# Weight splits written five half units ahead, expert output written in its own expert, and a pinned end

## The chip, the cores and the metric

The kernel runs on one core of one Trainium2 chip. The metric is the time of one execution on the device, in microseconds (us); three executions were timed, and their median counts. Engines are named as in the profile: PE is TensorE (PEld its weight loads), DVE is VectorE, ACT is ScalarE, POOL is GpSimd, SP is SyncE, which issues DMAs.

## The reference

One encoder block on x of 1024 positions by 1024 channels, in float32. A mixer (Fourier groups beside a gated short convolution) comes first; the change does not touch it. Then 16 experts follow, each of which takes the 128 positions with its highest router probability:

```python
probs = softmax(h @ w_router + b_router)
vals, idx = top_k(swapaxes(probs, 1, 2), 128)      # per expert: 128 positions
xe = h[idx]                                        # 128 x 1024
a = xe @ w_gate_e ; u = xe @ w_up_e                # 1024 x 2048 each
y = (silu(a) * u) @ w_down_e                       # 2048 x 1024
x[idx] += gate_f * (y * vals)
return rms_norm(x, g_final)
```

Weights are 25 MB an expert, and each is used once.

## The kernel before, in words

The kernel is written in a framework that plans the order of each engine when the kernel is built: a list scheduler walks through planned time, and among the instructions whose inputs and buffers are ready in the plan the one that was written first goes first. On the chip each engine then runs its own list in that order, and semaphores make it wait for others. `issue_after(i)` tells the planner that what is written inside comes after i in its engine's order.

Experts run one after the other (`expert`, L1176). An expert has 24 weight units of 1 MB: `raw` tiles of 128 x 2048, fetched by SP (`fetch`, L1107, issue at L1120) in a fixed list (`ulist`) into a ring of 7 + 4 + 1 = 12 buffers; the next unit is fetched when one has been split. A unit has two halves of 128 x 1024. Each half is split for precision (`split`, both lines recorded as L92 and L93): ACT copies it rounded into `whi` (L92), DVE subtracts for the rest, `wlo` (L93). Both have six buffers (`NWB`). A half is then used by 6 or more matmuls on TensorE of 512 columns: hi x hi, hi x lo, lo x hi (L1300 to L1302 for a and u, L106 to L112 for y).

The order in which an expert is written: for each of four column blocks fc, `up` (L1185) makes a of 512 columns from four halves, `put` (L1200) transposes the former block's product (L1205) and splits it into hth and htl, `up` makes u, then Silu of a (L1243, ACT) and the product h (L1244, DVE); in block 1 the next expert is chosen (`pick`: one-hot oh on DVE L1068, eight small matmuls L1075, the gather on POOL L1087); `down` (L1218) adds the former block's part to y. `unit` (L1147) writes the two instructions of a half's split right in front of that half's matmuls. At the end `turn` transposes the next expert's gathered rows (L1104). The weighed output ys (L1269, DVE) and its scatter with add to x2 in memory (L1270, POOL) are kept in a list, `self.left`, and written inside the next expert's first `up`, after its first unit.

The last expert has three units that are used unsplit in float32 (`plain`, matmuls L1222), with the transposed product copied into `htf` (L1209). Instead of scattering, it reads its rows of x2 early, and other rows of x2 are fetched as four more units at the places of `FIN` in the list; each is normed and written out (`final`: squares on ACT L1313, fms on DVE L664, frs on POOL L666, scaling on DVE L1318). The end group (L1282 to L1295) makes the last y in three column groups: h0 to h2 (L1286), add0 to add2 into xg (L1287), squares on ACT (L1288), gl0 to gl2 with g_final (L1289), the sum (L1291), ems and ers (L664, L666), the scaling and the output.

Of the kernel before, what the change touches and what calls it, by code (L numbers as in the profile page):

```python
# [6 lines left out]
F32 = mybir.dt.float32  # L7
# [4 lines left out]
OP = mybir.AluOpType  # L12
# [15 lines left out]
NWS, NWB = 3, 6  # L28
NSH = 0
NCMP = 2  # L30
FIN = ((10, 0), (8, 2), (6, 4), (4, 6))


def host_tables():
# [46 lines left out]
class Block:  # L81
# [575 lines left out]
            for _ in range(n):  # L657
                self.nc.tensor.matmul(t[:, 0:P], lhsT=self.ident, rhs=self.ident, start=True, stop=True)

    def rstd(self, pool, ss, name):  # L660
        nc = self.nc
        n = ss.shape[1]
        ms = pool.tile([P, n], F32, name=name + "ms")
        nc.vector.tensor_scalar(ms, ss, 1.0 / D, EPS, op0=OP.mult, op1=OP.add)  # L664
        rs = pool.tile([P, n], F32, name=name + "rs", bufs=2)
        nc.gpsimd.tensor_tensor(rs, ms, self.neghalf[:, 0:n], op=OP.pow)  # L666
        return rs

    def posdft(self, pool, v, row, cos, r, m, nm):

# [468 lines left out]
    def plain(self, rows):  # L1139

        raw = self.take().rearrange("p (i k n) -> p i k n", i=2, k=rows // 2)
        for i in range(2):
            yield raw[:, i]
            if i:
                self.fetch()
            self.step()

    def unit(self, rows):

        raw = self.take()  # L1150
        nc = self.nc
        for i in range(2):
            hi = self.wsp.tile([P, 1024], F32R, name="whi")
            lo = self.wsp.tile([P, 1024], F32R, name="wlo")
            src = raw[:, 1024 * i:1024 * i + 1024]
            if self.npop < NWS:
                nc.scalar.activation(hi, src, AF.Copy)
                with self.tc.issue_after(self.after):
                    nc.vector.tensor_tensor(lo, src, hi, op=OP.subtract)
            elif self.npop < NWB:  # L1160
                with self.tc.issue_after(self.hold):
                    self.split(hi, lo, src)
            else:
                self.split(hi, lo, src)
            self.npop += 1
            if i:
                if self.npop <= NWS:
                    with self.tc.issue_after(self.gather):
                        self.fetch(nc.gpsimd)
                else:  # L1170
                    self.fetch()
            self.pin = self.last
            self.step()
            yield hi.rearrange("p (k n) -> p k n", k=rows // 2), lo.rearrange("p (k n) -> p k n", k=rows // 2)

    def expert(self, pool, e, picked, side):  # L1176

# [7 lines left out]
        def up(fc, name):  # L1185
            ps = self.pau.tile([P, 512], F32, name=name)
            k = 0
            for b in range(2):
                for j, (wh, wl) in enumerate(self.unit(4)):
                    if self.npop > NWB and (j == 0 or self.ranked < 2):  # L1190
                        with self.tc.issue_after(self.hold):
                            next(side, None)
                    for i in range(2):
                        self.mm3x(ps, (xh[:, k, :], xl[:, k, :]), (wh[:, i, :], wl[:, i, :]), k == 0, k == KD - 1)
                        k += 1
                if self.left:
                    self.left.pop()()
            return ps

        def put(fc):  # L1200

            pt = self.ptp.tile([P, 4, P], F32, name="tp")
            h = hs.pop(fc)
            for i in range(4):
                nc.tensor.transpose(pt[:, i, :], h[:, i * P:(i + 1) * P], self.ident)  # L1205
            hf = None
            if last and fc in (1, 2):
                hf = pool.tile([P, 4, P], F32, name="htf")
                nc.scalar.activation(hf, pt, AF.Copy)  # L1209
                if fc == 2:  # L1210
                    ht[fc] = (None, None, hf)
                    return
            hh = pool.tile([P, 4, P], F32R, name="hth", bufs=2)
            hl = pool.tile([P, 4, P], F32R, name="htl", bufs=2)
            self.split(hh, hl, pt)
            ht[fc] = (hh, hl, hf)

        def down(fc, b):  # L1218
            if last and (fc, b) in ((1, 1), (2, 0), (2, 1)):
                for i, w in enumerate(self.plain(2)):  # L1220
                    for n in (0, 512):
                        nc.tensor.matmul(y[:, n:n + 512], lhsT=ht[fc][2][:, 2 * b + i, :], rhs=w[:, 0, n:n + 512],  # L1222
                                         start=False, stop=False)
                return
            for i, (wh, wl) in enumerate(self.unit(2)):
                if i == 0:
                    next(side, None)
                f = 4 * fc + 2 * b + i
                self.mm3([y[:, 0:512], y[:, 512:1024]], [t[:, 2 * b + i, :] for t in ht[fc][0:2]],
                         [(wh[:, 0, n:n + 512], wl[:, 0, n:n + 512]) for n in (0, 512)],  # L1230
                         first=(f == 0), last=(f == 15))

        for fc in range(4):
            pa = up(fc, "a")
            if last and fc == 0:
                self.gl = pool.tile([P, D], F32, name="ys")
                nc.gpsimd.dma_start(out=self.gl, in_=self.io["g_final"].rearrange("(o d) -> o d", o=1)
                                    .partition_broadcast(P))
            if fc:
                put(fc - 1)  # L1240
            pu = up(fc, "u")
            h = pool.tile([P, 512], F32, name="h", bufs=2)
            nc.scalar.activation(h, pa, AF.Silu)  # L1243
            nc.vector.tensor_tensor(h, pu, h, op=OP.mult)  # L1244
            hs[fc] = h
            if fc == 1:
                if last:
                    xg = pool.tile([P, D], F32, name="xg")
                    nc.gpsimd.indirect_dma_start(out=xg, out_offset=None, in_=self.x2_d,
                                                 in_offset=bass.IndirectOffsetOnAxis(ap=idx[:, 0:1], axis=0))  # L1250
                else:
                    while self.ranked < e + 2:
                        next(side, None)
                    with self.tc.issue_after(self.after):
                        nxt = self.pick(pool, e + 1)
            if fc:
                down(fc - 1, 0)
                if fc == 3:
                    put(3)
                down(fc - 1, 1)  # L1260
# [3 lines left out]
        if not last:  # L1264
            down(3, 1)

            def add():
                ys = pool.tile([P, D], F32, name="ys")
                nc.vector.scalar_tensor_tensor(ys, in0=y, scalar=val, in1=self.gf, op0=OP.mult, op1=OP.mult)  # L1269
                nc.gpsimd.indirect_dma_start(out=self.x2_d,  # L1270
                                             out_offset=bass.IndirectOffsetOnAxis(ap=idx[:, 0:1], axis=0),
                                             in_=ys, in_offset=None, compute_op=OP.add)
                self.scattered = e == NE - 2

            self.left.append(add)
            return nxt
        w = list(self.unit(2))
        for _ in range(8):
            self.step()
        ss = pool.tile([P, 3], F32, name="sse")  # L1280
        for n, cs in enumerate((slice(0, 512), slice(512, 768), slice(768, 1024))):
            for i, (wh, wl) in enumerate(w):  # L1282
                self.mm3x(y[:, cs], [t[:, 2 + i, :] for t in ht[3][0:2]], (wh[:, 0, cs], wl[:, 0, cs]), False, i == 1,
                          skip_group_check=n == 2)
            h = pool.tile([P, 512], F32, name="h", bufs=2)[:, 0:cs.stop - cs.start]
            nc.vector.scalar_tensor_tensor(h, in0=y[:, cs], scalar=val, in1=self.gf[:, cs], op0=OP.mult, op1=OP.mult)  # L1286
            nc.vector.tensor_tensor(xg[:, cs], xg[:, cs], h, op=OP.add)  # L1287
            nc.scalar.activation(h, xg[:, cs], AF.Square, accum_out=ss[:, n:n + 1])  # L1288
            nc.vector.tensor_tensor(xg[:, cs], xg[:, cs], self.gl[:, cs], op=OP.mult)  # L1289
        st = pool.tile([P, 1], F32, name="sst")  # L1290
        nc.vector.tensor_reduce(st, ss, axis=AX.X, op=OP.add)  # L1291
        rs = self.rstd(pool, st, "e")
# [31 lines left out]
    def run(self):  # L1324
# [92 lines left out]
        for i, t in FIN:  # L1417
            self.ulist.insert(len(self.ulist) - i, (None, NE - 1, P * t, P * t + 256, 0, D))
        self.nfetch, self.npop, self.units, self.rows = 0, 0, [], []
        def last():  # L1420
            return self.merge_out(m, KD - 1, *mg)

# [49 lines left out]
        side = self.route_rest(mp)  # L1472
        picked = self.turn(mp, *picked)
        self.hold = self.turned
        self.left = []
# [25 lines left out]
```

## Time and profile before

| what | value |
|---|---|
| median of 3 runs | 1948.76 us (1948.51 to 1949.74) |
| profiled execution | 1944.46 us, its span 1942.6 us, mean granted clock 0.992 |
| PE / PEld / DVE / ACT / POOL busy, share of the span | 97% / 78% / 82% / 58% / 7% |
| raw weights, issue to landing, median | 7.2 us (gate), 9.1 (up), 8.1 (down), 1 MB each |
| DMA | 549.02 MB, 283 GB/s over the span |

The experts begin at 775.76 us of the span. A matmul's record overlaps the next one's, so the busy share of PE is not its use. PEclk is the granted clock of TensorE as a share of full speed; a wait is shown in brackets behind an instruction, with the one that ended it.

### The profile page before, as it was taken

To read this page: it belongs to the slowest core of one execution; us is meant where nothing else is said; L and a number is where in the kernel's file an instruction comes from. 1 tells how busy PE (TensorE), PEld (TensorE's weight loads), DVE (VectorE), ACT (ScalarE), POOL (GpSimd) and SP (SyncE) were. 2 spreads that over 40 slices of the span, in tenths; PEclk is the share of its full clock that TensorE was granted. 3 is DMA by queue.
4 is the path that set the end of the run, shared out by engine and by line. 5 is a ranking of instruction groups with operands and counts; after the bars stand their busy time and mean duration, and the time that the engine had idled before them with its cause. 6 is when DMAs were issued, how large, how long until landed. Compare 5 with 4: busy or idle time off the path is not lost.

```text
span 1942.6 us, 23945 instructions
## 1 busy us (share of the span) xinstructions
PE 1888.7 (97%) x8777; PEld 1507.7 (78%) x8777; DVE 1583.4 (82%) x2005; ACT 1117.6 (58%) x1403; POOL 136.2 (7%) x124
## 2 busy tenths in 40 slices
PE   6999999999999999999999999999999999999996
PEld 5788888777788877777888777777778778777873
DVE  5976678676853767999999898898998999989886
ACT  5533233433510433776787777777767777677764
POOL 1000000000130111000000000000000000000001
PEclk9999999999999999999999999999999999999998
DMA  8322224465774842999999999999999999999993
GB/s 298 128 67 65 87 76 154 143 228 195 232 250 140 291 180 108 396 367 346 378 372 389 354 359 376 372 364 360 392 364 355 386 366 361 380 373 355 392 367 135
DMA packets 244746, 549.02 MB, mean 283 GB/s; under 512 B 12644, under 2 KB 51652, under 8 KB 244628
## 3 DMA queue, kind: packets, MB, share of 16 engines
q1 hardware_dynamic: 229248, 494.50, 69.8%
q0 software_dynamic: 14528, 52.75, 8.6%
q8 instruction: 69, 1.13, 0.2%
q10 hardware_dynamic: 852, 0.24, 0.1%
q14 instruction: 49, 0.40, 0.1%
HBM read 507.61 MB, written 39.86 MB: 282 GB/s over the span
## 4 chain that ended last, share of the span: by engine, by line
PE 76%; DVE 12%; DMA 5%; issue 4%; ACT 2%; POOL 0%; ACTq 0%; POOLq 0%; DVEq 0%
PE pb L315 9%; DVE wlo L93 7%; PE pa L315 6%; PE pc L315 6%; PE u L1302 5%; PE u L1300 5%; PE u L1301 5%; PE y L106 5%; PE y L109 4%; PE y L112 4%; PE a L1302 4%; PE a L1301 4%; PE a L1300 4%; DMA raw<-in_w_up_e_dram 3%; PE mm L106 3%
## 5 line engine op out<-in xcount | busy, mean ns | idle before, releaser
L93 DVE TENSOR_TENSOR wlo<-raw,whi 128x1024 fp32r<-128x1024 f32 x759 | 889.0, 1218 | 61.1 <-ACT whi L92 52.5
L92 ACT ACTIVATE whi<-raw 128x1024 fp32r<-128x1024 f32 x759 | 751.4, 1052 | 61.2 <-PE y L112 21.6
L1302 PE MATMUL a<-wlo,xh 128*128 128x512 f32 x512 | 206.2, 403 | 7.0 <-DVE wlo L93 5.7
L1302 PE MATMUL u<-wlo,xh 128*128 128x512 f32 x512 | 203.6, 398 | 2.4 <-DVE wlo L93 2.4
L1300 PE MATMUL u<-whi,xh 128*128 128x512 f32 x512 | 202.5, 395 | 1.6 <-ACT whi L92 1.6
L1300 PE MATMUL a<-whi,xh 128*128 128x512 f32 x512 | 201.5, 394 | 1.9 <-ACT whi L92 1.6
L1301 PE MATMUL a<-whi,xl 128*128 128x512 f32 x512 | 201.8, 394 | 0.0
L1301 PE MATMUL u<-whi,xl 128*128 128x512 f32 x512 | 201.8, 394 | 0.0
L109 PE MATMUL y<-wlo,hth 128*128 128x512 f32 x496 | 161.3, 406 | 0.5 <-DVE wlo L93 0.3
L106 PE MATMUL y<-whi,hth 128*128 128x512 f32 x496 | 159.5, 402 | 0.0
L112 PE MATMUL y<-whi,htl 128*128 128x512 f32 x496 | 156.4, 396 | 0.0
L92 ACT ACTIVATE wh<-s 128x512 fp32r<-128x512 f32 x80 | 50.3, 631 | 135.9 <-PE pc L315 76.0
L1302 PEld LDWEIGHTS a<-wlo,xh 128*128 128x128 f32 x512 | 96.4, 188 | 39.3 <-DVE wlo L93 19.8
L1302 PEld LDWEIGHTS u<-wlo,xh 128*128 128x128 f32 x512 | 96.3, 188 | 31.1 <-DVE wlo L93 8.0
L1300 PEld LDWEIGHTS a<-whi,xh 128*128 128x128 f32 x512 | 96.7, 189 | 21.9 <-ACT whi L92 2.5
L1301 PEld LDWEIGHTS a<-whi,xl 128*128 128x128 f32 x512 | 96.5, 188 | 22.0 <-DVE xl L93 0.4
L1300 PEld LDWEIGHTS u<-whi,xh 128*128 128x128 f32 x512 | 96.5, 188 | 21.0 <-ACT whi L92 2.6
L1301 PEld LDWEIGHTS u<-whi,xl 128*128 128x128 f32 x512 | 96.6, 189 | 20.5
L112 PEld LDWEIGHTS y<-whi,htl 128*128 128x128 f32 x496 | 93.4, 189 | 22.5
L106 PEld LDWEIGHTS y<-whi,hth 128*128 128x128 f32 x496 | 91.8, 189 | 20.9 <-issue 0.5
L109 PEld LDWEIGHTS y<-wlo,hth 128*128 128x128 f32 x496 | 89.9, 190 | 20.4 <-DVE wlo L93 2.4
L1243 ACT ACTIVATE h<-a 128x512 f32<-128x512 f32 x64 | 38.2, 596 | 106.6 <-PE a L1302 106.6
(530 smaller groups left out, 3183.1 us busy)
## 6 DMA issues: line engine op xcount, KB each, us to landing
raw<-in_w_gate_e_dram SPq DMA_DIRECT2D x126, 1024.0 KB, 7.2
raw<-in_w_up_e_dram SPq DMA_DIRECT2D x126, 1024.0 KB, 9.1
raw<-in_w_down_e_dram SPq DMA_DIRECT2D x126, 1024.0 KB, 8.1
ld<-in_w_ada_dram SPq DMA_DIRECT2D x48, 512.0 KB, 5.4
ld<-in_w_in_dram SPq DMA_DIRECT2D x44, 512.0 KB, 4.4
sg_d<-q POOLq DMA_DIRECT2D x8, 1024.0 KB, 6.1
ld<-sg_d SPq DMA_DIRECT2D x16, 512.0 KB, 4.9
x<-in_x_dram SPq DMA_DIRECT2D x8, 512.0 KB, 3.3
```

Of the source, the lines that this page charges most:

```text
L92: a = self.nc.scalar.activation(hi, src, AF.Copy).ins
L93: self.last = a, self.nc.vector.tensor_tensor(lo, src, hi, op=OP.subtract).ins
L106: nc.tensor.matmul(o, lhsT=lh, rhs=rh, start=first, stop=False)
L109: nc.tensor.matmul(o, lhsT=lh, rhs=rl, start=False, stop=False)
L112: nc.tensor.matmul(o, lhsT=ll, rhs=rh, start=False, stop=last)
L315: nc.tensor.matmul(o, lhsT=x[:, k, :], rhs=y[:, k, :], start=first and k == 0 and i == 0, stop=last and k == 3 and i == 2, skip_group_chec ...
L1243: nc.scalar.activation(h, pa, AF.Silu)
L1300: nc.tensor.matmul(o, lhsT=lhs[0], rhs=rhs[0], start=first, stop=False, **kw)
L1301: nc.tensor.matmul(o, lhsT=lhs[1], rhs=rhs[0], start=False, stop=False, **kw)
L1302: nc.tensor.matmul(o, lhsT=lhs[0], rhs=rhs[1], start=False, stop=last, **kw)
```

## The change

- `half` and `unit`: splits are written ahead of use. A queue takes halves until six stand in it, so five half units are written in front of the matmuls of a half. Plain halves stand in the queue too; `free` fetches the next unit in the order of the list of units.
- Silu of a is written right after a, in front of `put` and of u.
- ys and the scatter are written at the end of their own expert; `self.left` is gone.
- `htf` has two buffers.
- `FIN`: the first three of the four units of rows come 2, 1 and 1 units later in the list; `PICK` and `PLAIN` name values that are the same as before.
- In the end group the DVE operations are pinned in the order h0, add0, gl0, h1, add1, gl1, h2, add2, sum, ems, gl2.

```diff
-FIN = ((10, 0), (8, 2), (6, 4), (4, 6))
+PICK = 1
+FIN = ((8, 0), (7, 2), (5, 4), (4, 6))
+PLAIN = ((1, 1), (2, 0), (2, 1))
...
+    def half(self):
...
+        rows, plain = self.plan[self.nunit]
+        i = self.nhalf
+        if i == 0:
+            self.raw = self.take()
+        src = self.raw[:, 1024 * i:1024 * i + 1024]
+        if plain:
+            parts = [src]
...
+        self.queue.append([x.rearrange("p (k n) -> p k n", k=rows // 2) for x in parts])
+        if i:
+            if not plain:
+                self.free(self.nunit)
+            self.nunit += 1
+        self.nhalf = 1 - i
+        self.step()
...
+    def free(self, n):
+
+        self.read.add(n)
+        while self.nfree in self.read:
+            self.nfree += 1
+            if self.nfree == 1:
+                with self.tc.issue_after(self.gather):
+                    self.fetch(self.nc.gpsimd)
+            else:
+                self.fetch()
+
+    def unit(self):
+
+        for i in range(2):
+            while len(self.queue) < NWB and self.nunit < len(self.plan):
+                self.half()
+            self.nused += 1
+            yield self.queue.pop(0)
...
-                if self.left:
-                    self.left.pop()()
...
-                hf = pool.tile([P, 4, P], F32, name="htf")
+                hf = pool.tile([P, 4, P], F32, name="htf", bufs=2)
...
             pa = up(fc, "a")
+            h = pool.tile([P, 512], F32, name="h", bufs=2)
+            nc.scalar.activation(h, pa, AF.Silu)
...
             pu = up(fc, "u")
-            h = pool.tile([P, 512], F32, name="h", bufs=2)
-            nc.scalar.activation(h, pa, AF.Silu)
...
-            def add():
-                ys = pool.tile([P, D], F32, name="ys")
...
-            self.left.append(add)
+            ys = pool.tile([P, D], F32, name="ys")
+            nc.vector.scalar_tensor_tensor(ys, in0=y, scalar=val, in1=self.gf, op0=OP.mult, op1=OP.mult)
...
-            nc.vector.scalar_tensor_tensor(h, in0=y[:, cs], scalar=val, in1=self.gf[:, cs], op0=OP.mult, op1=OP.mult)
-            nc.vector.tensor_tensor(xg[:, cs], xg[:, cs], h, op=OP.add)
+            with tc.issue_after(order):
+                nc.vector.scalar_tensor_tensor(h, in0=y[:, cs], scalar=val, in1=self.gf[:, cs], op0=OP.mult,
+                                               op1=OP.mult)
+            order = nc.vector.tensor_tensor(xg[:, cs], xg[:, cs], h, op=OP.add).ins
             nc.scalar.activation(h, xg[:, cs], AF.Square, accum_out=ss[:, n:n + 1])
-            nc.vector.tensor_tensor(xg[:, cs], xg[:, cs], self.gl[:, cs], op=OP.mult)
+            if n < 2:
+                with tc.issue_after(order):
+                    order = nc.vector.tensor_tensor(xg[:, cs], xg[:, cs], self.gl[:, cs], op=OP.mult).ins
...
+        rs, order = self.rstd(pool, st, "e", True)
+        with tc.issue_after(order):
+            nc.vector.tensor_tensor(xg[:, cs], xg[:, cs], self.gl[:, cs], op=OP.mult)
```

## Rows read from the trace of the kernel before

**Rows 1.** Windows of experts 1, 2, 8, 15: busy us by engine, PEclk, DMA share, GB/s.

```profile
849.56:928.44 78.88, 75.65 (x373) 58.92 (x372) 75.77 (x106) 55.25 (x58) 5.43 (x2) 0.96 0.98 349
928.44:997.79 69.35, 69.35 (x321) 56.61 (x320) 65.77 (x65) 55.39 (x58) 3.88 (x2) 1.00 1.04 382
...
1350.18:1421.22 71.04, 70.31 (x322) 56.11 (x321) 64.11 (x64) 51.45 (x59) 3.63 (x2) 1.00 1.02 370
...
1846.38:1930.00 83.62, 76.29 (x299) 54.49 (x297) 66.31 (x67) 52.57 (x69) 8.46 (x7) 0.96 0.77 283
```

**Rows 2.** Groups by line, 1060 to 1770 us: busy us, mean ns | idle before.

```profile
L93 DVE TENSOR_TENSOR wlo<-raw,whi 128x1024 fp32r<-128x1024 f32 x480 | 557.4, 1217 | 37.9 <-ACT whi L92 37.6
...
L1302 PE MATMUL a<-wlo,xh 128*128 128x512 f32 x320 | 129.1, 403 | 5.4 <-DVE wlo L93 4.3
L1302 PE MATMUL u<-wlo,xh 128*128 128x512 f32 x320 | 127.1, 397 | 1.6 <-DVE wlo L93 1.6
```

**Rows 3.** PE in order of time, expert 8: start, us, instruction [idle before].

```profile
1353.19 0.39 PE L1301 MATMUL a<-whi,xl 128*128 128x512 f32 x1
1354.01 0.50 PE L1302 MATMUL a<-wlo,xh 128*128 128x512 f32 x1 [0.43 <-DVE wlo L93]
```

**Rows 4.** DVE in order of time, expert 8.

```profile
1351.55 1.28 DVE L1269 SCALAR_TENSOR_TENSOR ys<-y,val,gf 128x1024 f32<-128x1024 f32 x1
...
1369.35 1.22 DVE L1068 TENSOR_TENSOR oh<-pos,slot 128x1024 bf16<-128x1024 f32 x1
```

**Rows 5.** ACT in order of time, expert 8; xN are N instructions in a row.

```profile
1356.62 0.60 ACT L1243 ACTIVATE h<-a 128x512 f32<-128x512 f32 x1 [2.75 <-PE a L1302]
...
1368.58 7.69 ACT L92 ACTIVATE whi<-raw 128x1024 fp32r<-128x1024 f32 x8
1380.87 0.60 ACT L92 ACTIVATE hth<-tp 128x512 fp32r<-128x512 f32 x1 [4.60 <-PE tp L1205]
```

**Rows 6.** PE in order of time, expert 1, at the choice of the next expert.

```profile
895.75 0.38 PE L1075 MATMUL tp<-v,oh 128*128 128x5 bf16 x8 [2.85 <-DVE oh L1068]
```

**Rows 7.** DVE in order of time at the same place.

```profile
894.48 1.22 DVE L1068 TENSOR_TENSOR oh<-pos,slot 128x1024 bf16<-128x1024 f32 x1
```

**Rows 8.** PE in order of time, last expert.

```profile
1896.36 0.50 PE L1300 MATMUL a<-whi,xh 128*128 128x512 f32 x1 [1.63 <-ACT whi L92]
...
1906.43 0.50 PE L1300 MATMUL u<-whi,xh 128*128 128x512 f32 x1 [1.63 <-ACT whi L92]
```

**Rows 9.** ACT in order of time, last expert.

```profile
1894.77 0.60 ACT L1209 ACTIVATE htf<-tp 128x512 f32<-128x512 f32 x1 [7.00 <-PE y L1222]
...
1896.21 1.05 ACT L1313 ACTIVATE oh<-raw 128x1024 bf16<-128x1024 f32 x1
...
1904.83 0.60 ACT L1243 ACTIVATE h<-a 128x512 f32<-128x512 f32 x1 [3.60 <-PE a L1302]
```

**Rows 10.** Windows after those two waits, columns as in rows 1.

```profile
1898.50:1901.90 3.40, 3.30 (x9) 2.10 (x8) 2.99 (x5) 2.73 (x4) 0.21 (x1) 0.50 0.85 341
1908.70:1912.10 3.40, 3.13 (x8) 2.01 (x7) 2.99 (x5) 3.40 (x5) 0.28 (x1) 0.50 0.70 282
```

**Rows 11.** DVE in order of time, end group.

```profile
1928.65 0.48 DVE L1286 SCALAR_TENSOR_TENSOR h<-y,val,gf 128x256 f32<-128x256 f32 x1 [0.34 <-PE y L1302]
...
1929.51 0.68 DVE L1289 TENSOR_TENSOR xg<-xg,ys 128x512 f32<-128x512 f32 x1
1930.21 0.48 DVE L1286 SCALAR_TENSOR_TENSOR h<-y,val,gf 128x256 f32<-128x256 f32 x1
1930.61 0.41 DVE L1289 TENSOR_TENSOR xg<-xg,ys 128x256 f32<-128x256 f32 x1
...
1932.52 0.15 DVE L664 TENSOR_SCALAR ems<-sst 128x1 f32<-128x1 f32 x1
```

**Rows 12.** ACT in order of time, end group: the first square's read.

```profile
1928.88 0.19 ACT L1288 ACTIVATION_READ_ACCUMULATOR h<-xg 128x1 f32 x1
```

**Rows 13.** POOL in order of time, end group.

```profile
1932.75 0.56 POOL L666 TENSOR_TENSOR ers<-ems,neghalf 128x1 f32<-128x1 f32 x1 [15.37 <-DVE ems L664]
```

More of the change, by code (lines that the diff above doesn't have):

```diff
@@ L658, in warm, with rstd @@
                 self.nc.tensor.matmul(t[:, 0:P], lhsT=self.ident, rhs=self.ident, start=True, stop=True)
-    def rstd(self, pool, ss, name):
+    def rstd(self, pool, ss, name, tell=False):
         nc = self.nc
@@ L663, in rstd @@
         ms = pool.tile([P, n], F32, name=name + "ms")
-        nc.vector.tensor_scalar(ms, ss, 1.0 / D, EPS, op0=OP.mult, op1=OP.add)
+        i = nc.vector.tensor_scalar(ms, ss, 1.0 / D, EPS, op0=OP.mult, op1=OP.add).ins
         rs = pool.tile([P, n], F32, name=name + "rs", bufs=2)
         nc.gpsimd.tensor_tensor(rs, ms, self.neghalf[:, 0:n], op=OP.pow)
-        return rs
+        return (rs, i) if tell else rs
     def posdft(self, pool, v, row, cos, r, m, nm):
@@ L1137, in step @@
                 next(r, None)
[L1139 to L1150, printed above, removed]
-        nc = self.nc
-        for i in range(2):
+    def half(self):
+        nc = self.nc
+        rows, plain = self.plan[self.nunit]
[6 more added lines that the diff above has]
+        else:
             hi = self.wsp.tile([P, 1024], F32R, name="whi")
             lo = self.wsp.tile([P, 1024], F32R, name="wlo")
-            src = raw[:, 1024 * i:1024 * i + 1024]
+            parts = [hi, lo]
             if self.npop < NWS:
@@ L1164, in unit @@
                 self.split(hi, lo, src)
+                self.pin = self.last
             self.npop += 1
[L1166 to L1174, printed above, removed]
+        self.queue.append([x.rearrange("p (k n) -> p k n", k=rows // 2) for x in parts])
[12 more added lines that the diff above has]
+                    self.fetch(self.nc.gpsimd)
+            else:
+                self.fetch()
[5 more added lines that the diff above has]
+            yield self.queue.pop(0)
     def expert(self, pool, e, picked, side):
@@ L1188, in up @@
             for b in range(2):
-                for j, (wh, wl) in enumerate(self.unit(4)):
-                    if self.npop > NWB and (j == 0 or self.ranked < 2):
+                for j, (wh, wl) in enumerate(self.unit()):
+                    if self.nused > NWB and (j == 0 or self.ranked < 2):
                         with self.tc.issue_after(self.hold):
@@ L1218, in down @@
         def down(fc, b):
-            if last and (fc, b) in ((1, 1), (2, 0), (2, 1)):
-                for i, w in enumerate(self.plain(2)):
+            if last and (fc, b) in PLAIN:
+                for i, (w,) in enumerate(self.unit()):
                     for n in (0, 512):
@@ L1223, in down @@
                                          start=False, stop=False)
+                self.free(24 * e + (24 - 2 * (4 - fc) + b if fc == 3 else 6 * fc + 8 + b))
                 return
-            for i, (wh, wl) in enumerate(self.unit(2)):
+            for i, (wh, wl) in enumerate(self.unit()):
                 if i == 0:
@@ L1241, in expert @@
             pu = up(fc, "u")
-            h = pool.tile([P, 512], F32, name="h", bufs=2)
-            nc.scalar.activation(h, pa, AF.Silu)
             nc.vector.tensor_tensor(h, pu, h, op=OP.mult)
             hs[fc] = h
-            if fc == 1:
+            if fc == PICK:
                 if last:
@@ L1265, in expert @@
             down(3, 1)
-            def add():
-                ys = pool.tile([P, D], F32, name="ys")
[L1269 to L1273, printed above, removed]
-            self.left.append(add)
+            ys = pool.tile([P, D], F32, name="ys")
+            nc.vector.scalar_tensor_tensor(ys, in0=y, scalar=val, in1=self.gf, op0=OP.mult, op1=OP.mult)
+            nc.gpsimd.indirect_dma_start(out=self.x2_d, out_offset=bass.IndirectOffsetOnAxis(ap=idx[:, 0:1], axis=0),
+                                         in_=ys, in_offset=None, compute_op=OP.add)
+            self.scattered = e == NE - 2
             return nxt
-        w = list(self.unit(2))
+        w = list(self.unit())
         for _ in range(8):
@@ L1280, in expert @@
         ss = pool.tile([P, 3], F32, name="sse")
+        tc, order = self.tc, self.pin[1]
         for n, cs in enumerate((slice(0, 512), slice(512, 768), slice(768, 1024))):
@@ L1285, in expert @@
             h = pool.tile([P, 512], F32, name="h", bufs=2)[:, 0:cs.stop - cs.start]
-            nc.vector.scalar_tensor_tensor(h, in0=y[:, cs], scalar=val, in1=self.gf[:, cs], op0=OP.mult, op1=OP.mult)
-            nc.vector.tensor_tensor(xg[:, cs], xg[:, cs], h, op=OP.add)
+            with tc.issue_after(order):
+                nc.vector.scalar_tensor_tensor(h, in0=y[:, cs], scalar=val, in1=self.gf[:, cs], op0=OP.mult,
+                                               op1=OP.mult)
+            order = nc.vector.tensor_tensor(xg[:, cs], xg[:, cs], h, op=OP.add).ins
             nc.scalar.activation(h, xg[:, cs], AF.Square, accum_out=ss[:, n:n + 1])
-            nc.vector.tensor_tensor(xg[:, cs], xg[:, cs], self.gl[:, cs], op=OP.mult)
+            if n < 2:
+                with tc.issue_after(order):
+                    order = nc.vector.tensor_tensor(xg[:, cs], xg[:, cs], self.gl[:, cs], op=OP.mult).ins
         st = pool.tile([P, 1], F32, name="sst")
         nc.vector.tensor_reduce(st, ss, axis=AX.X, op=OP.add)
-        rs = self.rstd(pool, st, "e")
+        rs, order = self.rstd(pool, st, "e", True)
+        with tc.issue_after(order):
+            nc.vector.tensor_tensor(xg[:, cs], xg[:, cs], self.gl[:, cs], op=OP.mult)
         nc.vector.tensor_scalar(xg[:, 0:512], xg[:, 0:512], rs, None, op0=OP.mult)
@@ L1419, in run @@
         self.nfetch, self.npop, self.units, self.rows = 0, 0, [], []
+        self.plan = []
+        for e in range(NE):
+            for f in range(5):
+                self.plan += [(4, False)] * (4 if f < 4 else 0)
+                self.plan += [(2, e == NE - 1 and (f - 1, b) in PLAIN) for b in range(2 if f else 0)]
+        self.nunit, self.nhalf, self.nfree, self.nused, self.queue, self.read = 0, 0, 0, 0, [], set()
         def last():
@@ L1474, in run @@
         self.hold = self.turned
-        self.left = []
         for e in range(NE):
```

## The prediction

> **What bounds the kernel now.** I read the profile's busy table first, then the windows cut at expert boundaries, then the groups of instructions by line, the instructions in order of time on each engine, and last the waits and the chain that ended last. The busy table says that TensorE is busy for 97% of the span; in this kernel that says little, since a matmul's record runs on while the next one starts. The windows say more [rows 1]. Experts 2 and 3 take 69.35 us each: this is what the matmuls and transposes of one expert need at full clock, and I use it as the floor. Experts 5 to 13, nine of them, take 70.97 to 71.04 us; one row stands for all. So a steady expert lies 71.04 - 69.35 = 1.69 us above the floor, nine of them 15.2 us. VectorE is busy 64.11 of 71.04 us, ScalarE 51.45: neither is the bound as a total. The DMA engines show a full share in every row, but they showed it at 69.35 us too, with a higher rate (382 against 370 GB/s), so transfers are not the bound either.
>
> Where the 1.69 us sit is told by the groups by line [rows 2]: the only matmuls that are held up are those that read wlo, the small part of a split, and what they wait for is the subtraction on VectorE. One of them is seen in TensorE's order [rows 3]: two matmuls start 0.82 us apart where the rate is 0.23 (0.59 lost); the other places of an expert, one in u and one in a, share the remaining 1.1. Beside the first there is a reason on VectorE: the expert output ys (1.28 us) runs just before the subtraction that TensorE needs, and before the second the one-hot oh of the next expert's choice (1.22) [rows 4]. On ScalarE [rows 5] Silu of a starts at 1356.62, although the kernel writes it after all splits of u, and further on eight splits run in one piece. So the order on the engines is not the order in which the kernel writes things; it comes from when the planner has each input ready, and splits stand in it by when their weight unit arrives in the plan.
>
> Two other places lie above the floor. Expert 1 takes 78.88 us at a mean clock of 0.96 [rows 1]; inside it TensorE stands for 2.85 us in front of the choice of the next expert, waiting for oh [rows 6], which VectorE starts only at 894.48 behind ranking work and splits [rows 7]. The last expert takes 83.62 us to 1930, also at 0.96. There TensorE waits twice for a split on ScalarE, 1.63 us each [rows 8]; before the first, ScalarE's copy into htf waited 7.00 us for plain matmuls that still read the only htf buffer, and the split that TensorE needed was queued behind it; before the second it was Silu that waited, 3.60 us [rows 9]. [...]
>
> **The change part by part.** Work before the experts is untouched: 0.
>
> Splits written five half units ahead. No instruction is added or removed; 48 splits an expert remain, 1.217 us on VectorE [rows 2]. The fetch of a unit moves with its splits, SP's queue keeps its order of units, and the ring of raw buffers keeps its size, so the DMAs are the same. What the edit alters is precedence: among instructions that are ready in the plan, splits now come before oh, ys, the h product and htl where they came behind. From below: the three waits go in nine experts, -15.2. From above: in nine experts one such operation falls behind one split more, and its whole 1.22 us shows, +11.0. I take 0, the value nearest to what [rows 5] show: in the steady experts a split's place is set by the plan's arrival of its unit, so writing it earlier can't bring it forward, and the six pairs of split buffers hold no more than before. Silu written ahead of u: 0, since it runs there already [rows 5]; if a split now goes in front of it, it is late by one split's copy, some 1 us, while its product waits for u anyway.
>
> ys and the scatter written in their own expert. ys keeps its 1.28 us, and its input is complete at the same moment. It now stands behind all splits written up to there, but in front of the next expert's later ones; before, it was written after the next expert's second half unit or so. At best the 0.59 us in front of it goes (nine times, 5.3), at worst it holds y, and the next expert's first y matmul is far behind. POOL, 7% busy, only moves a scatter forward in its queue in front of the next gather; nothing waits for it until rows are read at the end. I take 0: the slack moves from one wlo to another.
>
> Expert 1's oh. From below, the wait (2.85) and the clock loss of that expert (4% of 78.88 = 3.2) both go: -6.0. From above, two splits more go before oh: +2.4. The middle is -1.8; VectorE is busy 75.77 of 78.88 us there, so most of a wait that goes comes back as another. I take -1.5.
>
> Second htf buffer. The copy need not wait for the plain matmuls, so the 7.00 us wait on ScalarE can go and splits run during them. From below, both waits and both stretches of half clock go: 2 x 1.63 + 2 x 3.4 x 0.5 = -6.7. From above, 0: the copy waits instead for its transposes, and the next splits for buffers. The second wait hangs on Silu, not on htf, so I take part of the first alone: -2.0.
>
> Rows of the final norm. They are read up to two units later, in the same number. One row pair costs ScalarE 2 x 1.05 us of squares [rows 9] and VectorE a similar amount, and this work now meets the splits of the last a and u in a denser stretch. Between 0 (ScalarE has idle time there: 52.57 of 83.62) and one row's 2.5 with its reads; I take +1.5.
>
> Pins of the last operations. Now gl0 runs between h1 and h2 [rows 11]; it is pinned in front of h1, and it has to wait for the square of the first part, whose read ends at 1928.88 + 0.19 = 1929.07 [rows 12]. With 0.68 for gl0 (0.05 of it overlapped) h1 starts at 1929.70 instead of 1928.65. Then gl1 (0.41) has to wait for the second square too: add1 ends 0.9 after h1 starts, the square takes 0.6, so gl1 starts near 1931.15 and h2 near 1931.57. From h2 to ems it was 2.31 us, with gl1 and gl2 inside; without these two (0.33 each when pipelined) it is 1.65, so ems comes at 1933.2 instead of 1932.52: +0.7. From below it is -0.7 (gl1 and gl2 out of the way and no wait); nothing hides it, since POOL's ers and the output follow directly [rows 13].
>
> Sum: 0 + 0 - 1.5 - 2.0 + 1.5 + 0.7 = -1.3. The profiled execution took 1944.46 us (span 1942.6), 4.3 under the median of the runs, 1948.76. So 1943.2 for an execution like the profiled one, and 1947.5 as a median.
>
> **Rivals.** A, the forecast: the plan's order in the steady experts stays; 1947.5, own range 1942 to 1953.
>
> B: the look-ahead works. The waits for wlo go and experts 5 to 13 fall to the floor that experts 2 and 3 reach: 1947.5 - 15.2 = 1932. For it: raw weights land 7 to 9 us after their issue by the DMA table of the page, with a ring of twelve units, so the data is there; VectorE has 7 us free an expert. Against it: experts 2 and 3 reach the floor already with the old order of writing, so that order isn't what fails later.
>
> C, slower: precedence of splits pushes one operation of TensorE's feedback path (h product, htl, Silu) behind one more split. hth on ScalarE waited 4.60 us for transposes while the splits behind it stood [rows 5]; if the product that feeds the transposes is later by 1.22, the split behind hth is later too, and TensorE, which already waits for that split, feels nearly all of it. It decides from the point where the product ends later than the y matmuls in front of its transposes. Price 9 x 1.22 = 11.0: 1958. Against it: the planner may place transposes later instead. [...]
>
> D: the htf edit gives all it can, -6.7 instead of -2.0: 1942.8. For it: the wait is long and its releaser is named. Against it: half of the loss is behind Silu.
>
> That the change doesn't do what it says is in A: an order of writing that the plan doesn't follow.
>
> **How the numbers follow.** A 0.40, B 0.17, C 0.26, D 0.14, other 0.03. A measurement of this kernel tells about 0.2% (3.9 us) from no change. Faster: B whole, most of D, a little of A: 0.33. Same: most of A and a little of C and D: 0.41. Slower: most of C and a little of A: 0.26. The range 1931 to 1959 takes in B's and C's centres; less than 2 in 10 lies outside. Cases of both signs hold most of the chance, so A's own range, 1942 to 1953, stands beside it.
>
> **What would show it.** Right: windows of experts 5 to 13 still near 71.0, with waits for wlo at the same places; htf's wait on ScalarE gone; h1 about 1 us later than the end of the first square's record now allows, ems some 0.7 later counted from the last full y group. B shows as nine windows at 69.4, C as nine windows at 72 and more with longer waits of hth and TensorE stops at transposes. It would be wrong if the planner reorders splits throughout, or if the last expert's splits come late for their buffers.

## The result

The changed kernel takes 1960.74 us (median of 4, 1958.17 to 1961.09) against 1948.80 for the kernel before: a ratio of 1.0058, 95% interval 1.0040 to 1.0075. It is slower by 11.9 us. The forecast was 1947.5 with a range to 1959, so it missed on the slow side; what happened in the steady experts is rival C, by its mechanism and nearly by its price.

The windows of the profiled execution (span 1959.0, time 1960.79) show where. Experts 0, 1, 2, 8 and the last in the changed kernel, columns as in [rows 1]; the last window is cut at the same length as there:

```profile
782.21:859.72 77.51, 75.26 (x401) 58.85 (x401) 75.39 (x116) 56.59 (x60) 1.32 (x1) 0.98 1.04 394
859.72:934.17 74.45, 72.56 (x371) 57.23 (x372) 72.73 (x105) 54.52 (x58) 4.42 (x2) 1.00 0.97 349
934.17:1003.51 69.34, 69.34 (x322) 56.61 (x320) 65.78 (x65) 55.38 (x58) 3.87 (x2) 1.00 1.03 378
1359.02:1431.02 72.00, 70.64 (x322) 56.11 (x321) 64.28 (x64) 51.34 (x59) 7.03 (x2) 1.00 1.02 365
1861.99:1945.61 83.62, 73.66 (x293) 51.78 (x291) 65.95 (x66) 52.08 (x67) 7.78 (x7) 1.00 0.77 286
```

Expert 2 still takes the floor. A steady expert (expert 8) takes 72.00 us in place of 71.04, though DVE and ACT have the same work. From boundary to boundary the two profiled spans differ as follows (changed minus before): the experts begin 6.45 later (782.21 against 775.76); experts 0 and 1 together -0.71; 2 to 4 +0.07; 5 to 13 +8.94; 14 +0.87; the last to its last full y group -0.05; from there to the end +0.92. Without the first, 10.0. That first one is no effect of the change: PE, DVE, ACT and POOL run the same instructions in the same order ahead of the experts, and 4.65 of the 6.45 us arise between 450 and 530 us of the span, where this execution has 10.2 us at a granted clock of 0.50 and that of before has none. In the 14 profiled executions of this study the experts begin between 775.76 and 789.37, the profiled execution of before being the earliest.

What costs expert 8 these 0.96 us (the nine lose 0.99 in the mean) is read from VectorE. The kernel before in expert 8, around the product of the first column block (start, us, instruction, [idle before]):

```profile
1358.20 3.50 DVE L93 TENSOR_TENSOR wlo<-raw,whi 128x1024 fp32r<-128x1024 f32 x3 [0.84 <-ACT whi L92]
1362.13 0.69 DVE L1244 TENSOR_TENSOR h<-u,h 128x512 f32<-128x512 f32 x1 [0.44 <-PE u L1302]
1362.74 3.49 DVE L93 TENSOR_TENSOR wlo<-raw,whi 128x1024 fp32r<-128x1024 f32 x3
```

The same place in the changed kernel, where the split's lines are L94 and L95 and the product's is L1260:

```profile
1367.01 4.63 DVE L95 TENSOR_TENSOR wlo<-raw,whi 128x1024 fp32r<-128x1024 f32 x4 [0.83 <-ACT whi L94]
1371.56 0.68 DVE L1260 TENSOR_TENSOR h<-u,h 128x512 f32<-128x512 f32 x1
1372.16 2.35 DVE L95 TENSOR_TENSOR wlo<-raw,whi 128x1024 fp32r<-128x1024 f32 x2
```

Four splits stand in front of the product where three stood, and two behind it where there were three. Counted over the trace, one split of the part that follows ran in front of each product of experts 5 to 13; in the changed kernel it is two, in all four column blocks. Before, VectorE was free and waited 0.44 us for u, though ScalarE had ended the copy for the next split at 1361.01; now the product waits behind that split. On TensorE the transposes of h follow it; before and after:

```profile
1361.71 0.39 PE L1302 MATMUL u<-wlo,xh 128*128 128x512 f32 x1
...
1363.77 0.60 PE L1205 MATMUL tp<-ident,h 128*128 128x128 f32 x4
```

```profile
1370.52 0.39 PE L1321 MATMUL u<-wlo,xh 128*128 128x512 f32 x1
...
1373.96 0.60 PE L1220 MATMUL tp<-ident,h 128*128 128x128 f32 x4
```

From the last matmul of u to the transposes it was 2.06 us, eight matmuls of the next a; now it is 3.44, with fourteen. The product itself starts 0.62 us later, counted from that matmul; the transposes are 1.38 later, since they stand six matmuls (one half unit) further back in TensorE's order. ScalarE's hth, which waits for them with the next splits queued behind it, ends its wait later too. ACT before, then after:

```profile
1364.40 0.60 ACT L92 ACTIVATE hth<-tp 128x512 fp32r<-128x512 f32 x1 [1.50 <-PE tp L1205]
```

```profile
1374.59 0.60 ACT L94 ACTIVATE hth<-tp 128x512 fp32r<-128x512 f32 x1 [2.88 <-PE tp L1220]
```

On VectorE, htl needs hth and has splits behind it. It ran without a wait; now it waits, and the next split does too. DVE before, then after:

```profile
1366.14 0.68 DVE L93 TENSOR_TENSOR htl<-tp,hth 128x512 fp32r<-128x512 f32 x1
```

```profile
1375.22 0.69 DVE L95 TENSOR_TENSOR htl<-tp,hth 128x512 fp32r<-128x512 f32 x1 [0.71 <-ACT hth L94]
1376.17 2.36 DVE L95 TENSOR_TENSOR wlo<-raw,whi 128x1024 fp32r<-128x1024 f32 x2 [0.26 <-ACT whi L94]
```

What TensorE loses by it: the wait in u that was short becomes the longest, and one in the last a is new (PE, changed kernel):

```profile
1380.10 0.39 PE L1320 MATMUL u<-whi,xl 128*128 128x512 f32 x1
1381.19 0.50 PE L1321 MATMUL u<-wlo,xh 128*128 128x512 f32 x1 [0.70 <-DVE wlo L95]
...
1407.35 0.40 PE L1320 MATMUL a<-whi,xl 128*128 128x512 f32 x1
1407.84 0.50 PE L1321 MATMUL a<-wlo,xh 128*128 128x512 f32 x1
```

These two starts are 1.09 us apart, 0.86 over the rate of 0.23 at which matmuls of 512 columns start one after the other where none waits (from 1378.72 to 1380.10 in the same trace); in the kernel before the same wait cost 0.34. The second pair is 0.49 apart, 0.26 over it. That is 0.52 and 0.26 more than before; two further starts 0.34 apart, in place of 0.23, make up the rest of the 0.96. The wait in front of which ys runs [rows 3, 4] is as it was: 0.60 for 0.59.

### The profile page after: what moved, and what is told of

Read it like the earlier page. It is cut to its first block, busy times and chain, and to the rows that moved or that the text cites. A ratio compares the mean times of both kernels' runs of the same rounds, so it can differ in the third digit from the quotient of the medians.

```text
span 1959.0 us, 23969 instructions
## 1 busy us (share of the span) xinstructions
PE 1893.9 (97%) x8777; PEld 1509.4 (77%) x8777; DVE 1585.5 (81%) x2005; ACT 1116.1 (57%) x1403; POOL 147.8 (8%) x124
## 4 chain that ended last, share of the span: by engine, by line
PE 71%; DVE 12%; DMA 9%; issue 4%; ACT 3%; POOL 1%; ACTq 0%; POOLq 0%; SPq 0%; DVEq 0%
PE pb L317 9%; DVE wlo L95 8%; PE pa L317 6%; PE pc L317 6%; PE a L1321 5%; DMA raw<-in_w_gate_e_dram 5%; PE u L1321 4%; PE u L1320 4%; PE u L1319 4%; PE a L1320 4%; PE a L1319 4%; PE y L108 3%; PE y L114 3%; PE mm L114 3%; PE y L111 3%
## 5 line engine op out<-in xcount | busy, mean ns | idle before, releaser
L95 DVE TENSOR_TENSOR wlo<-raw,whi 128x1024 fp32r<-128x1024 f32 x759 | 889.4, 1218 | 69.2 <-ACT whi L94 62.6
L94 ACT ACTIVATE whi<-raw 128x1024 fp32r<-128x1024 f32 x759 | 752.0, 1052 | 63.7 <-PE a L1320 20.2
L94 ACT ACTIVATE wh<-s 128x512 fp32r<-128x512 f32 x80 | 50.3, 631 | 135.3 <-PE pc L317 69.3
L94 ACT ACTIVATE hth<-tp 128x512 fp32r<-128x512 f32 x63 | 37.6, 597 | 155.0 <-PE tp L1220 154.8
```

What stands on the lines that cost most here:

```text
L94: a = self.nc.scalar.activation(hi, src, AF.Copy).ins
L95: self.last = a, self.nc.vector.tensor_tensor(lo, src, hi, op=OP.subtract).ins
```

## The experiments

Theory P: one more split that is written ahead of the h product runs in front of it, and product, transposes and hth are late. Rivals: S, the early Silu or ys in its own expert does it; R, transfers, or the longer look-ahead as such. x1 to x3 are the changed kernel with one edit each, x4 undoes two parts of it.

**x1_ahead1**, splits written one half unit ahead:

```diff
-            while len(self.queue) < NWB and self.nunit < len(self.plan):
+            while len(self.queue) < 2 and self.nunit < len(self.plan):
```

> The changed kernel with splits written one half unit ahead in place of five; all other parts of the change stay. Theory P (a split written ahead of the h product runs in front of it, product, transposes and hth are late): the product's place in the order is that of the kernel before again, steady experts 5 to 13 return from 72.0 to 71.0 us, in all some 9 to 10 us less than the changed kernel, about 1951. Rival S (the early Silu or ys in its own expert does it): windows stay at 72.0 and the time at 1960. Rival R (transfers or the other runs' scatter): 1960 too, with any window.

1951.36 us, ratio to before 1.0017 (1.0000 to 1.0035). Expert 8:

```profile
1363.55:1434.81 71.26, 70.29 (x322) 56.11 (x320) 64.13 (x64) 51.44 (x59) 3.62 (x2) 1.00 1.01 370
```

P's place and size. One split is still written ahead of the product, but it is the one that ran in front of it before the change too, and the orders around the product are those of the kernel before. The 0.22 over 71.04 come with ys, which now stands one split earlier in front of the wait in a; that part was not expected. Nor was this: the last expert up to its last full y group took 74.46 us, against 79.86 in the changed kernel and 79.91 before. So the time met the expected 1951 partly by luck: these 5.4 us are largely made up for by the 0.22 in nine experts and by 2.7 us that TensorE is late after 100 us of the span, ahead of all that the edit touches (see the last section).

**x2_ahead2**, the same line with 3 (two half units ahead).

> As the changed kernel, with splits written two half units ahead. Theory P: two is enough for one split to come in front of the h product, so steady windows are 72.0 us and the time that of the changed kernel, 1958 to 1961: a step between one and two, and none between two and five. A rival by which the loss grows with the look-ahead (more buffers held, more work in front) gives a time between, near 1954, with windows near 71.3.

1962.53 us, 1.0082 (1.0063 to 1.0100):

```profile
1359.41:1431.41 72.00, 70.63 (x321) 56.08 (x320) 64.29 (x64) 51.34 (x59) 3.62 (x2) 1.00 1.01 363
```

A step, as P has it: two half units cost as much as five, and the orders on VectorE, ScalarE and TensorE in expert 8 are those of the changed kernel. A loss that grows with the look-ahead is out.

**x3_drain**, five ahead, but inside u nothing of a later part is written until the product stands (one split of it is written during a already, as many as x1 has):

```diff
-            while len(self.queue) < NWB and self.nunit < len(self.plan):
+            while len(self.queue) < NWB and self.nunit < len(self.plan if upto is None else self.plan[:upto]):
...
         def up(fc, name):
+            upto = self.nused // 2 + 2 if name == "u" else None
...
-                for j, (wh, wl) in enumerate(self.unit()):
+                for j, (wh, wl) in enumerate(self.unit(upto)):
```

> The changed kernel, five half units ahead, but while u is made no split of a later part is written until the h product stands. Theory P: this alone brings steady windows back to 71.0 us and the time to about 1951. If look-ahead itself costs (raw buffers released in another rhythm, ScalarE filled with early splits), windows stay at 72.0 and the time near 1960.

1947.36 us, 0.9998 (0.9984 to 1.0013). Expert 8:

```profile
1358.91:1429.96 71.05, 70.29 (x322) 56.11 (x320) 64.14 (x64) 51.47 (x59) 3.62 (x2) 1.00 1.01 370
```

With five ahead everywhere but at the product, the whole loss is gone, and expert 8 has the orders of the kernel before on VectorE, ScalarE and TensorE. Look-ahead as such costs a steady expert nothing, and gives it nothing. The last expert's stretch is 74.26 here too.

**x4_silu_ys_back**, Silu behind u and ys in the next expert again, the rest of the change kept:

```diff
             pu = up(fc, "u")
+            h = pool.tile([P, 512], F32, name="h", bufs=2)
+            nc.scalar.activation(h, pa, AF.Silu)
...
+            self.left.append(add)
```

> The changed kernel with Silu written behind u again and ys with its scatter in the next expert, as before the change; five half units ahead, pins, rows and htf of the change stay. Theory P: windows stay at 72.0 us, time 1958 to 1961. Rival S: windows 71.0, time about 1951.

1959.21 us, 1.0061 (1.0045 to 1.0076); expert 8 takes 72.03. S is out.

**x6_one_htf**, **x7_no_pins**, **x8_rows_back**: the other terms of the sum, each undone alone (the three edits in this order), read from the last expert's stretches in one profiled execution.

```diff
-                hf = pool.tile([P, 4, P], F32, name="htf", bufs=2)
+                hf = pool.tile([P, 4, P], F32, name="htf")
...
-            with tc.issue_after(order):
-                nc.vector.scalar_tensor_tensor(h, in0=y[:, cs], scalar=val, in1=self.gf[:, cs], op0=OP.mult,
-                                               op1=OP.mult)
+            nc.vector.scalar_tensor_tensor(h, in0=y[:, cs], scalar=val, in1=self.gf[:, cs], op0=OP.mult, op1=OP.mult)
...
-FIN = ((8, 0), (7, 2), (5, 4), (4, 6))
+FIN = ((10, 0), (8, 2), (6, 4), (4, 6))
```

> The changed kernel with one htf buffer. The engines' orders are the same; only the wait for the buffer differs. If the second buffer frees the splits of the last a, as the sum had it (2.0 us), the last expert is 1 to 4 us longer with one buffer, and ScalarE's htf copy waits some 7 us for plain matmuls. If not, the last expert's time is the same within 0.3 us.

79.86 us to the last full y group, as with two buffers: the second buffer gives nothing here.

> The changed kernel without the pins of the last VectorE operations. The sum had the pins at +0.7 us, as gl0 waits for the first square in front of h1: the time from the last full y group to the end of the span then shrinks from 17.2 to about 16.4 us, all else stays. If the pins are free it stays at 17.2.

From the last full y group to the end 16.26 us in place of 17.18, as in the kernel before: the pins cost 0.92. Other kernels with the pins take 17.18 to 17.56, those without 16.25 to 16.27.

> The changed kernel with the units of rows at their old places in the list. The sum had the later rows at +1.5 us: the stretch of the last expert up to its last full y group shrinks by 1 to 2 us. If later rows cost nothing, it stays within 0.3 us; if it was the places that helped, it grows.

79.97 in place of 79.86: the later rows do nothing here.

**x9_ahead1_one_htf** and **x10_ahead1_rows_back**: the same two edits made in x1, to see what its 5.4 us in the last expert are.

> The kernel with splits one half unit ahead (x1), whose last expert took 74.5 us to its last full y group against 79.9 in the changed kernel, now with one htf buffer; the engines' orders are those of x1. Theory P for the end: the second htf buffer pays only while the transposes in front of it are early, and five half units ahead made them late; so here taking it away costs most of the 5.4 us, 78 to 80. If the 5.4 us come from the splits' order alone and not from htf, the stretch stays at 74.5.

78.80 in place of 74.46. The second buffer is worth 4.34 us, but only where the transposes lead. In x1 four of them (tp) run among the y matmuls at 1903.76, ahead of the plain ones. In the changed kernel they stand behind eight records of plain matmuls, and ACT's htf waits for them instead of for the buffer. It is the late product that puts them there: x3, whose one edit brings the product forward, takes 74.26. PE and ACT of the changed kernel, then of x1:

```profile
1906.32 3.59 PE L1237 MATMUL y<-raw,htf 128*128 128x512 f32 x8
1909.76 0.60 PE L1220 MATMUL tp<-ident,h 128*128 128x128 f32 x4
```

```profile
1910.39 0.60 ACT L1224 ACTIVATE htf<-tp 128x512 f32<-128x512 f32 x1 [7.79 <-PE tp L1220]
```

```profile
1903.76 0.60 PE L1220 MATMUL tp<-ident,h 128*128 128x128 f32 x4
```

```profile
1904.40 0.60 ACT L1224 ACTIVATE htf<-tp 128x512 f32<-128x512 f32 x1 [3.43 <-PE tp L1220]
```

And of x9, where the order is x1's and the one buffer is what it waits for:

```profile
1904.89 0.60 ACT L1224 ACTIVATE htf<-tp 128x512 f32<-128x512 f32 x1 [7.78 <-PE y L1237]
```

> x1 with the units of rows at their old places. If the later rows share in the 5.4 us of the last expert, its stretch grows from 74.5 towards 80; if they cost, as the sum had it (+1.5), it shrinks to 73; if they do nothing, as they did with five half units ahead, it stays.

78.91 in place of 74.46. The later rows are worth 4.45 us where the sum had a cost of 1.5. With the rows at their old places two splits stand ahead of htf on ACT, not four, and y waits for one behind it (PE, x10):

```profile
1894.63 0.66 PE L1220 MATMUL tp<-ident,h 128*128 128x128 f32 x4 [0.78 <-DVE h L1260]
1896.92 0.74 PE L108 MATMUL y<-whi,hth 128*128 128x512 f32 x2 [1.63 <-ACT whi L94]
```

So the gain of the last expert needs three things at once: product early, second buffer, later rows. Any one missing gives 78.8 to 80. All these kernels have the early Silu; whether it shares in the gain, no run shows.

**x5_three_moves**, the kernel before with the three small operations moved that stand beside its waits:

```diff
-                if self.left:
-                    self.left.pop()()
+                if self.left and name == ("a" if last else "u"):
+                    with self.tc.issue_after(self.last[1]):
+                        self.left.pop()()
...
+        with self.tc.issue_after(self.prod or self.after):
+            nc.vector.tensor_tensor(oh, pos.to_broadcast([P, ST, P]),
...
-            if fc:
+            if fc and fc != 2:
                 put(fc - 1)
...
-                if fc == 3:
-                    put(3)
+                if fc in (1, 3):
+                    put(fc)
```

> The kernel before with three operations moved in the steady experts, each found beside one of the three waits for wlo: ys behind the second split of u (was between the splits of a), the one-hot oh of the next choice behind the last h product of the expert before, and the transposes of the second block written before the second half of the y matmuls in front of them. Theory P extended (what is lost in an expert is the order of small VectorE and TensorE work among the splits): experts 5 to 13 fall from 71.0 towards 69.35 us, in all 10 to 15 us, 1934 to 1939. If instead the pace is that of the transfers, as the full DMA share of those windows could mean, the windows stay at 71.0 and the time at 1948.

1938.05 us, 0.9932 (0.9919 to 0.9946). Expert 8:

```profile
1352.37:1422.33 69.96, 69.86 (x321) 56.41 (x320) 63.83 (x64) 51.32 (x59) 3.23 (x2) 1.00 1.02 375
```

The waits were the order of small work among the splits; what each of the three moves gives by itself was not run. The DMA share is 1.02 as before, at 375 GB/s against 370: a full share was no sign here that transfers set the pace.

**x11_best**: x5's three moves, no look-ahead, and of the change Silu early, two htf buffers and the later rows; no pins. **x12_best_early**: the same with `(NWB if self.nused < 90 else 1)` in place of the 1, that is five ahead in experts 0 and 1 alone.

```diff
-            while len(self.queue) < NWB and self.nunit < len(self.plan):
+            while len(self.queue) < 1 and self.nunit < len(self.plan):
```

> The parts that helped, together: the kernel before's order of splits, the three moves of x5, and from the change Silu early, the second htf buffer and the later rows; no pins. Theory P: steady experts at 69.95 us as in x5 (about 11 us under before), and the last expert's stretch near 74.5 (5.4 us under before): 1932 to 1934. If the two gains share a cause, it stays at x5's 1938.

1933.16 us, 0.9925 (0.9907 to 0.9943): 14.8 us faster than the kernel before and 27.6 faster than the changed one's 1960.74, which is from another set of runs. Expert 8 takes 69.99, the last expert to its last full y group 74.23, the end 16.25: both gains stand together in the stages, although the ratio's interval overlaps that of x5.

```profile
1840.71:1914.94 74.23, 70.37 (x286) 51.23 (x285) 63.30 (x62) 51.49 (x65) 8.34 (x7) 1.00 0.85 319
```

> x11 with splits written five half units ahead in experts 0 and 1 alone, where the changed kernel took 150.5 to 152.0 us for both against 152.7 before. If the look-ahead helps there by its own order, 1 to 2 us less than x11; if those differences are only between runs, the same as x11.

1932.26 us, 0.9922 (0.9901 to 0.9944). Experts 0 and 1 took 150.74 against 151.46 in x11, in one execution each; in time the two kernels are not told apart.

## Why the prediction was wrong

The step that failed is the first of its sum: "a split's place is set by the plan's arrival of its unit, so writing it earlier can't bring it forward", costed at 0. It measured +8.94 us. It was inferred from ScalarE's order [rows 5], and for ScalarE it was right: copies, Silu and hth stand in the same order before and after in a steady expert. It doesn't hold on VectorE: in front of each product two splits of the part that follows run in place of one. There splits pile up: the fourth split was ready 0.69 us before VectorE came free and still ran behind the product. That the plan then goes by which was written first is an inference from the scheduler's rule; the orders of x1 to x3 fit it, with one split in front of the product where one is written ahead and two where two or more are. The same paragraph names the h product among the operations that splits now come before and prices it, +11.0, as its upper bound; the 0 was taken from ScalarE's rows alone. The evidence was in the trace, in rows that the prediction didn't read: the product waiting 0.44 us for u with splits right behind it.

Rival C named this mechanism, operation and place, and priced it at 11.0 us for nine experts. Measured: 8.94 for these and 0.87 for expert 14. It got a chance of 0.26 where the sum had 0 as its value; its time, 1958, was short by 2.7. That the price came so near is luck in part: one operation by 1.22 us was priced, while in expert 8 the product is 0.6 us late in all four blocks and the transposes 0.9 to 1.4. The chain that C gives from the product to the split behind hth is what ScalarE's rows in expert 8 show: hth waits 2.88 us in place of 1.50, and the copy that runs right behind it starts 4.57 us after the start of the last matmul of u (1375.09) in place of 3.19 (1364.90).

The other terms, with what they measured:

- Experts 0 and 1, -1.5: -0.71 in the profiled execution of the changed kernel and -2.0 to -2.2 in x4 and x6 to x8, so sign and size were right. The mechanism held where it was looked for: the wait for oh and the 6.8 us at a clock of 0.50 behind it (894.97 to 901.80 before) are gone, and expert 1 takes 74.5 us in all five, 4.4 less. What the sum lacked is that expert 0 pays for it, 76.0 us in place of 73.80, with TensorE waiting 1.07 us for a ranking mask and 0.69 for hth near its end. In the changed kernel's execution it takes 77.51, with 3.4 us at a clock of 0.50 at its start that x4 and x6 to x8 don't have. Here the look-ahead did reach the engines: five splits of later parts run in front of every product of the two experts, where most had one.
- Second htf buffer, -2.0: 0.00. The wait of htf did not go: 7.00 us for plain matmuls became 7.79 for the transposes. The value of 4.34 is real, but it was lost to the late product. The prediction saw the upper bound's reason ("the copy waits instead for its transposes") and didn't tie it to the product's place; this makes C dearer than it was priced, by a gain that it prevents. The clock of 0.50 that its lower bound counted, twice 3.40 us [rows 10], had no price of its own there: behind the 1.63 us stop, x6 runs 3.4 us at 0.50 and the changed kernel none, and both take 79.86 us to the last full y group, as the changed kernel waits for wlo instead. The changed kernel, then x6 (columns as in [rows 1], the clock is the third from the end):

```profile
1913.50:1916.90 3.40, 3.06 (x12) 1.84 (x11) 2.19 (x2) 3.40 (x7) 0.00 (x0) 1.00 0.00 0
```

```profile
1908.20:1911.60 3.40, 3.40 (x10) 2.33 (x9) 2.35 (x3) 3.40 (x6) 0.21 (x1) 0.50 0.01 2
```

- Later rows, +1.5: -0.11 in the changed kernel, -4.45 where product and buffer allow it. The cost did not show, and where the rows do something the sign was wrong. What counted was not ScalarE's load but which splits stand ahead of htf.
- Pins, +0.7: +0.92. The mechanism is as worked out: gl0 waits 0.79 us for the first square and h1 stands behind it, 1.07 us later than before counted from the last full y group (1.05 was worked out), so that ems comes 0.8 us later by the same count. DVE, changed kernel, the end group:

```profile
1944.65 0.69 DVE L1306 TENSOR_TENSOR xg<-xg,ys 128x512 f32<-128x512 f32 x1 [0.79 <-ACT h L1303]
1945.26 0.48 DVE L1300 SCALAR_TENSOR_TENSOR h<-y,val,gf 128x256 f32<-128x256 f32 x1
...
1946.77 0.42 DVE L1306 TENSOR_TENSOR xg<-xg,ys 128x256 f32<-128x256 f32 x1 [0.58 <-ACT h L1303]
1947.11 0.48 DVE L1300 SCALAR_TENSOR_TENSOR h<-y,val,gf 128x256 f32<-128x256 f32 x1
...
1948.87 0.15 DVE L666 TENSOR_SCALAR ems<-sst 128x1 f32<-128x1 f32 x1
```

- ys in its own expert, early Silu, 0: 0 within the change (x4: 72.03 against 72.00).

Rival B (the look-ahead works) was out for the reason given against it: x3 shows five half units ahead at 71.05. Its gain was there to be had, by other means: x5 takes 1.08 of the 1.69 us per expert by moving ys, oh and the transposes, the operations that [rows 4] and [rows 5] show beside the waits.

## What to carry to other kernels

Before writing work ahead of its use, list for each engine what is ready when it comes free, and ask which instruction the early one will pass; where the early work runs only just ahead of its use, an operation on the way from one engine to the next and back (product, transposes, rounding) should not be among them. Where an engine waits a little for many small reasons, look at the small operation that runs just in front of each wait and move that one: three such moves gave 1.08 us an expert (x5), where a look-ahead of five half units gave nothing (x3). A buffer added against a named wait paid here only where the other input of the waiting instruction was early (4.34 us in x1, 0.00 in the changed kernel), so look at that one as well.

## What the runs showed that had not been expected

The cost is a step and not a slope: 71.26 us an expert with one half unit ahead, 72.00 with two and 72.00 with five. And it is no cost of a split in front of the product as such: in experts 2 and 3 four or five splits of later parts run in front of each product, before and after the change, and they take 69.3 us. From expert 5 on it is one before and two in the changed kernel. Why the order falls back in expert 4, no run shows. In the last expert the early product, the second buffer and the later rows were each worth 4 to 5 us with the other two in place (74.46 us with all, 78.80, 78.91 and 79.86 with one missing); the early product with just one of the others is only 1.0 to 1.1 us better than the 79.91 of the kernel before.

The profiled execution of the kernel before reached its experts 1.2 to 13.6 us earlier than any other of the 14. Part of that, in the changed kernel 4.65 of its 6.45 us, arises between 450 and 530 us, where its granted clock is 0.50 for 10.2 us and that of before is 1.00. Another part is in the kernels: in eight of them (x1 to x5, x8, x9, x12) two small VectorE operations near 65 us stand in the other order, and TensorE is 2.4 to 3.9 us later at 100 us than in the kernel before; in the other five it is -0.2 to 0.5. No edit touches that place. A difference between two single profiles is read stage by stage, not from their spans, and small differences between the times of these kernels are read with that in mind.
